# Attention operands split where they leave PSUM, keys turned by DMA, constants moved, and seven PSUM banks for output units

## The chip, the cores and the metric

The kernel is one program on one core of a Trainium2 chip. The core has TensorE (PE, with its weight loads shown apart as PEld), VectorE (DVE), ScalarE (ACT), GpSimd (POOL) and SyncE (SP). Each takes its own instructions in order. They meet through semaphores, and data comes and goes by DMAs, here nearly all issued from SP's queue. PE writes its results to PSUM, which has eight banks; DVE and ACT read them from there ("evacuate" them) into SBUF. The metric is the device time of the whole program in microseconds, lower is better.

## What is computed

The reference is one inference step of a decoder with two layers, on a prompt of 2048 tokens and on 8 sequences with 4 new tokens each (32 sample rows), with a model width of 1024:

```python
proj = h @ w_in                                   # layer 0; h = rmsnorm(x)
qa, fa, ia, ga, qb, kb, vb, gb, fb = _split(proj, [512]*4 + [512]*4 + [4])
o_a, s_a = gated_linear_chunked(...)              # linear attention with per-channel decay, 4 heads of 128
o_b = fox_attend(hb(qb), kb_h, vb_h, log_fb)      # softmax attention with forget bias, 4 heads of 128
out = concat([norm(o_a) * silu(ga), o_b * silu(gb)]) @ w_out
```

`fox_attend` on the prompt is causal attention with logits `q.k * scale + c_t - c_s`, where `c` is the running sum of log forget gates. On the samples it also reads 16 pages of 128 cached rows for each sequence. Layer 1 is another gated linear attention (GLA, 4 heads, keys of 128, values of 256), with its own input and output projections. The keys and values of layer 0 are outputs too, in fp32.

Every fp32 projection is done as three fp16 matmuls: each operand is split into a high part `hi = fp16(x)` and a low part `lo = fp16(x - hi)`, and `hi*hi + hi*lo + lo*hi` is accumulated in fp32 (`mm3`, lines 593 to 597). Attention does the same with Q, K, V and the probabilities.

## The kernel before, in words

The prompt is worked on in two halves of 1024 tokens; the 32 sample rows go with the first half. The stages follow each other on PE:

- Layer 0's input units (0 to 875 us in the profile). A unit is one block of 256 weight columns: fetch, measure, scale and split the weights, then project. `phase_even` runs 16 units for each half in the order v0 g0 qf0 qf1 Bq0 Bg0 v1 g1 qf2 qf3 Bq1 Bg1 Bk0 Bv0 Bk1 Bv1. `A` names belong to the linear attention, `B` names to softmax attention, and the last digit of B units is a pair of heads. Linear-attention heads (`lin_attn`) are mixed between the units by `mux`, which deals out the instructions of two generators by their costs: head 3 runs beside Bg1, Bk0 and Bv0.
- Softmax attention (875 to 1300 us). `fox_prompt` goes through 16 groups (a head and 512 query rows). `scores` computes logits and probabilities for four blocks of 128 rows, `values` transposes the probabilities on PE and multiplies them with V, one group behind. `fox_sample` is mixed in: it reads 256 pages of the cache through a pool of 25 buffers, turns the key pages on PE (`pkt`) and multiplies (`sc`, `pv`).
- Output units of layer 0 (1300 to 1500 us), then layer 1's input units with GLA heads, then its output units. Units 0 to 3 of a layer and half are `out_units(hf, layer)`.

The order inside an engine's queue is not written out by hand: a planner takes the traced instructions in order with a model of their durations, and `issue_after(x)` places the instructions traced inside it, those on x's engine, behind x. Tiles come from pools by tag with a number of buffers; a tile that reuses a buffer waits for its last readers.

The places that the change touches:

- `proj_tm` (line 608) projects with tokens on PSUM's partitions, two token tiles (256 rows) to a bank of tag `pj`; its `evac` callback moves the result out. There are three `pj` banks, two `gr`, two `o` and one `st`. The linear attention uses `gr`, `st` and `o`.
- `mk_bq` (line 980): Q's projection leaves PSUM by one ACT copy with a scale (line 990) and goes to DRAM in fp32 (`qTd`), already with the head's channels on partitions.
- `mk_bkv` (line 1000): K and V leave PSUM by one DVE multiplication (line 1019) into a `c2` tile (four buffers), which is stored as the output. V is stored a second time to `vd`. K is turned by four PE transposes per pair of tiles (line 1044) in a `gr` bank, leaves it by an ACT copy (line 1048) and is stored to `kTd`.
- In `fox_prompt`, `loads` (line 1348) fetches a group's Q, K and V in fp32 into `raw` tiles, issued while the group before is worked on, and `split` (line 1357) makes the fp16 parts: ACT copies, POOL subtracts (lines 1329 to 1331). V is also scaled on ACT. The splits stand behind the last exponential and the last turned key page.
- `more_consts` (line 162) makes masks and constants for later stages. It is traced inside the first unit after v0; on ACT its work stands behind the unit's second tanh, on DVE behind nothing.
- `out_units` (line 1805) runs `proj_tm` on `w_out`; DVE adds the residual (lines 1825 and 1831) as it empties the bank.

Of the kernel before, what the change touches and what calls it, by code (L numbers as in the profile page):

```python
# [123 lines left out]
class Kern:  # L124
    def __init__(self, ctx, tc, ins, outs):
        self.ctx, self.tc, self.nc = ctx, tc, tc.nc
        self.i, self.o = ins, outs
        self.loaded = {}


    def consts(self):
# [21 lines left out]
        self.qTd = dp.tile([NH, P, NTOK], F32, name="qTd")  # L153
        self.kTd = dp.tile([NH, P, NTOK], F32, name="kTd")
        self.sgd = dp.tile([NH, P, NTOK], F32, name="sgd")
        self.vd = dp.tile([NTOK, 512], F32, name="vd")
# [451 lines left out]
    def proj_tm(self, pps, act, W, hf, evac, nm, width=256, pairs=True):  # L608
# [3 lines left out]
        for g in range(0, len(tl), per):  # L612
# [6 lines left out]
            ps = pps.tile([P, per, width], F32, tag="pj", name=f"pt_{nm}{g}")  # L619
# [284 lines left out]
    def even_half(self, hf, act, wpool, wp, pps, npool, S):  # L904
# [95 lines left out]
        def mk_bkv(hp, which):  # L1000
# [3 lines left out]
            def run(W):  # L1004
# [5 lines left out]
                def ev(ps, g, cnt, m):  # L1010
# [5 lines left out]
                    if g % 2 == 0:  # L1016
                        held[:] = [wp.tile([P, 2, 256], F32, tag="c2", name=f"B{which}{hf}{hp}{g}")]
                    t = held[0]
                    nc.vector.tensor_scalar(t[:m, g % 2 : g % 2 + cnt], ps[:, :, :256], c, None, ALU.mult)
                    if m < P:  # L1020
                        dst = o[f"fox_{which}_s"][0].rearrange("b t h d -> (b t) (h d)")[:, cs]
                        nc.sync.dma_start(dst, t[:m, 0])
                        if which == "v":
                            nc.sync.dma_start(self.vd[T : T + TS, cs], t[:m, 0])
                    elif (g + cnt) % 2 == 0:
# [11 lines left out]
                    else:  # L1037
                        return
                    if which == "k":
                        pk = pps.tile([P, 2, 256], F32, tag="gr", name=f"BkT{hf}{hp}{g}")  # L1040
                        nt = 1 if m < P else 2
                        for j in range(2):
                            for c in range(nt):
                                nc.tensor.transpose(pk[:, j, c * P : c * P + m], t[:m, c, j * P : (j + 1) * P],
                                                    self.ident[:m, :m])
                        ks = wp.tile([P, 2, 256], F32, tag="c2", name=f"BkS{hf}{hp}{g}")
                        wd = nt * m
                        nc.scalar.activation(ks[:, :, :wd], pk[:, :, :wd], AF.Copy, scale=self.fsc["k", hp][0])
                        dc = T if m < P else hf * HALF + g * P
                        nc.sync.dma_start(  # L1050
                            self.kTd[2 * hp : 2 * hp + 2, :, dc : dc + wd].rearrange("h p t -> p h t"), ks[:, :, :wd])
# [23 lines left out]
    def phase_even(self):  # L1075
# [4 lines left out]
        with pool("act", side="right") as ap, pool("w", side="right") as w0, pool("wl", side="right") as wp1, \  # L1080
# [7 lines left out]
            self.scales2, self.ready, self.fsc, self.logit, self.v_undo = {}, {}, {}, {}, {}  # L1088
# [23 lines left out]
            for hf in range(2):  # L1112
# [11 lines left out]
                if hf == 0:  # L1124
# [26 lines left out]
                    with tc.issue_after(self.last_x.ins), tc.issue_after(self.last_a.ins), \  # L1151
                            tc.issue_after(self.last_th.ins):
# [146 lines left out]
    def phase_fox(self):  # L1299
# [5 lines left out]
        if True:  # L1305
            fx = Pool(f0, {"vh": 5, "vl": 5, "P": 17, "th": 4, "tl": 4, "sg": 3, "y": 1},
                      Pool(f1, {"raw": 6, "caus": 1, "qh": 2, "ql": 2, "kh": 5, "kl": 5, "cb": 2, "st1": 12, "cm": 2}))
# [9 lines left out]
    def load(self, fx, src, nm):  # L1317

        r = fx.tile([P, 512], F32, tag="raw", name=f"raw_{nm}")
        self.nc.sync.dma_start(r.rearrange("p (c d) -> p c d", d=src.shape[2]) if len(src.shape) == 3 else r, src)  # L1320
        return r

    def split(self, fx, r, nm, scale=None):

        nc = self.nc
        hi = fx.tile([P, 512], F16, tag=nm[0] + "h", name=f"h_{nm}")
        lo = fx.tile([P, 512], F16, tag=nm[0] + "l", name=f"l_{nm}")
        if scale is not None:
            nc.scalar.activation(r, r, AF.Copy, scale=scale)
        nc.scalar.activation(hi, r, AF.Copy)  # L1330
        nc.gpsimd.tensor_tensor(lo, r, hi, ALU.subtract)
        return hi, lo

    def fox_prompt(self, fx, pps, caus):

        nc = self.nc
        cbs, K, V, Q, SG, raw = {}, {}, {}, {}, {}, {}
# [10 lines left out]
        def loads(h, G):  # L1348
            gs = slice(G * 512, (G + 1) * 512)
            raw["q"] = self.load(fx, self.qTd[h][:, gs], f"q{h}{G}")  # L1350
            raw["k"] = self.load(fx, self.kTd[h][:, gs], f"k{h}{G}")
            bias(h, G)
            raw["v"] = self.load(fx, self.vd[gs, h * P : (h + 1) * P].rearrange("(c s) d -> s c d", s=P), f"v{h}{G}")
# [3 lines left out]
        def split(which, h, G):  # L1357

            with ExitStack() as st:
                for x in (self.last_exp, self.last_kt):  # L1360
                    if x is not None:
                        st.enter_context(self.tc.issue_after(x.ins))
                r = self.split(fx, raw[which], f"{which}{h}{G}", self.fsc["v", h // 2][0] if which == "v" else None)
# [825 lines left out]
```

## Time and profile before

| | us |
|---|---|
| median of 3 runs (2366.59 to 2371.02) | 2367.46 |
| the profiled execution | 2365.9 |
| its span in the trace | 2364.2 |
| PE busy in the span | 2265.2 |
| DVE busy | 1404.4 |
| ACT busy | 1090.3 |
| POOL busy | 818.6 |

The page gives the busy time of each engine, the costliest groups of instructions, and what each engine waited for. A matmul's end is modelled and neighbours overlap, so a matmul's listed duration (0.27 us for 128x256) is not the time that it takes from PE: the next one starts 0.109 us later. What PE loses is read from its idle time, and from the distance between starts. "Idle before, releaser" says which instruction ended the wait. TensorE's granted clock was 0.989 over the run.

### The profile page before, as it was taken

What the parts mean: (1) busy time and instruction counts of PE and PEld (TensorE: products, weight loads), DVE (VectorE), ACT (ScalarE), POOL (GpSimd) and SP (SyncE); (2) the same over time, 40 slices, a digit from 0 to 9 for tenths busy, and PEclk for the clock granted to TensorE, in tenths of its full rate; (3) what the DMA queues carried; (4) which work ended last, traced back from release to release, by engine and by line L of the source; (5) the groups of instructions that cost most, each with busy time, mean ns of one, the idle gap of its engine ahead of it and who ended that gap; (6) DMA issues with size and microseconds to landing.
All of it is one profiled execution on the core that took longest, in us unless ns stands there. A gap on an engine that the chain in (4) does not pass through costs nothing. (4 is left out here: it accounts for less than half of the span.)

```text
span 2364.2 us, 58202 instructions
## 1 busy us (share of the span) xinstructions
PE 2265.2 (96%) x23124; PEld 1613.1 (68%) x23124; DVE 1404.4 (59%) x3225; ACT 1090.3 (46%) x2372; POOL 818.6 (35%) x858
## 2 busy tenths in 40 slices
PE   6999999999999999999999999999899999999998
PEld 5667667864655875655445888777677666666887
DVE  6656557536664538666767444366675655557554
ACT  5434343333333226556667543436545545545333
POOL 3133324112212226234557345144452422222223
PEclk9999999999999999999999999999999999999999
DMA  6231334755441267776873867633234431115453
GB/s 191 73 89 59 100 109 146 196 157 148 145 123 56 75 196 239 239 256 198 280 239 117 278 197 249 148 96 108 79 117 101 107 103 57 48 55 166 152 194 149
DMA packets 358004, 344.89 MB, mean 146 GB/s; under 512 B 90994, under 2 KB 300723, under 8 KB 357731
## 3 DMA queue, kind: packets, MB, share of 16 engines
q1 hardware_dynamic: 356226, 336.64, 46.8%
q8 instruction: 182, 2.98, 0.5%
q0 software_dynamic: 1504, 4.52, 0.5%
q14 instruction: 92, 0.75, 0.1%
HBM read 248.73 MB, written 79.63 MB: 139 GB/s over the span
## 5 line engine op out<-in xcount | busy, mean ns | idle before, releaser
L595 PE MATMUL pt_o<-w_o,act 128*128 128x256 f16 x1024 | 281.1, 274 | 8.2 <-DVE xo L1825 6.6
L597 PE MATMUL pt_o<-w_o,act 128*128 128x256 f16 x1024 | 281.0, 274 | 3.8 <-DVE act L1784 3.7
L596 PE MATMUL pt_o<-w_o,act 128*128 128x256 f16 x1024 | 281.1, 275 | 1.5 <-POOL w_o L356 1.5
L597 PEld LDWEIGHTS <-act 128*128 128x128 f16 x2304 | 227.3, 99 | 39.4 <-DVE act L1784 5.1
L596 PEld LDWEIGHTS <-act 128*128 128x128 f16 x2304 | 227.3, 99 | 38.5 <-issue 8.4
L595 PEld LDWEIGHTS <-act 128*128 128x128 f16 x2304 | 227.4, 99 | 35.9 <-issue 3.4
L761 POOL TENSOR_TENSOR kA<-kA,fA 128x512 f32<-128x512 f32 (+1 forms) x56 | 79.5, 1419 | 190.1 <-PE gl_A L727 141.9
L595 PE MATMUL pt_Cv<-w_Cv,act 128*128 128x256 f16 (+1 forms) x512 | 141.4, 276 | 0.0
L597 PE MATMUL pt_Cv<-w_Cv,act 128*128 128x256 f16 (+1 forms) x512 | 141.3, 276 | 0.0
L596 PE MATMUL pt_Cv<-w_Cv,act 128*128 128x256 f16 (+1 forms) x512 | 141.3, 276 | 0.0
L761 POOL TENSOR_TENSOR kC<-kC,fC 128x512 f32<-128x512 f32 (+1 forms) x56 | 83.6, 1493 | 153.8 <-PE gl_C L727 102.5
L1392 ACT ACTIVATE L<-L,nm,kc 128x512 f32<-128x512 f32 (+3 forms) x160 | 118.2, 741 | 33.5 <-DVE nm L1390 27.8
L1400 POOL TENSOR_SCALAR L<-L,nm 128x512 f32<-128x512 f32 (+3 forms) x160 | 99.0, 632 | 64.5 <-DVE nm L1396 23.9
L1427 ACT ACTIVATE th<-pt 128x512 f16<-128x512 f32 (+3 forms) x159 | 80.5, 528 | 64.5 <-PE pt L1420 63.6
L1428 DVE TENSOR_TENSOR tl<-pt,th 128x512 f16<-128x512 f32 (+3 forms) x159 | 94.6, 609 | 21.4 <-ACT th L1427 20.5
L1420 PE MATMUL pt<-ident,L 128*128 128x128 f32 x544 | 91.2, 279 | 7.1 <-POOL L L1400 4.2
L1420 PEld LDWEIGHTS pt<-ident,L 128*128 128x128 f32 x544 | 66.6, 143 | 33.3 <-DVE tl L1428 8.3
L1544 PEld LDWEIGHTS pkt<-ident,pgcache_fox_k 128*128 128x128 f32 x512 | 57.4, 141 | 42.7 <-issue 25.1
L1877 ACT ACTIVATE vC<-pt_Cv,kc 128x512 f32<-128x512 f32 (+1 forms) x40 | 23.9, 598 | 129.9 <-PE pt_Cv L597 129.9
L1544 PE MATMUL pkt<-ident,pgcache_fox_k 128*128 128x128 f32 x512 | 75.1, 278 | 7.3 <-DVE kts L1548 5.1
L1825 DVE SCALAR_TENSOR_TENSOR xo<-pt_o,kc,xo 128x512 f32<-128x512 f32 x48 | 35.8, 748 | 62.0 <-PE pt_o L597 57.2
L597 PE MATMUL pt_Av<-w_Ai,act 128*128 128x256 f16 x256 | 70.9, 277 | 1.5 <-DVE act L591 1.5
(957 smaller groups left out, 6788.5 us busy)
## 6 DMA issues: line engine op xcount, KB each, us to landing
pgcache_fox_k<-in_cache_fox_k SPq DMA_DIRECT2D x128, 256.0 KB, 4.4
pgcache_fox_v<-in_cache_fox_v SPq DMA_DIRECT2D x128, 256.0 KB, 4.3
yr<-yT SPq DMA_DIRECT2D x16, 1024.0 KB, 7.2
x1d<-xo SPq DMA_DIRECT2D x48, 256.0 KB, 4.1
wr_Aqf<-in_w_in_even SPq DMA_DIRECT2D x64, 128.0 KB, 3.2
wr_o<-in_w_out_even SPq DMA_DIRECT2D x32, 256.0 KB, 6.0
xo<-in_x_prompt SPq DMA_DIRECT2D x32, 256.0 KB, 4.2
wr_Cv<-in_w_in_odd SPq DMA_DIRECT2D x32, 256.0 KB, 3.8
```

The lines of the kernel that those rows point to most:

```text
L595: nc.tensor.matmul(ps, lh[0], rh[0], start=first, stop=False)
L596: nc.tensor.matmul(ps, lh[0], rh[1], start=False, stop=False)
L597: return nc.tensor.matmul(ps, lh[1], rh[0], start=False, stop=last)
L761: nc.gpsimd.tensor_tensor(kv[:, :, 0], kv[:, :, 0], t1.to_broadcast([P, nb, w]), ALU.mult)
L1392: self.last_exp = nc.scalar.activation(lt[:, :w], lt[:, :w], AF.Exp, bias=nm[:, 0:1], scale=ib, accum_out=nm[:, 2 + j : 3 + j])
L1400: nc.gpsimd.tensor_scalar(lt[:, :w], lt[:, :w], nm[:, 1:2], 2.0**14, ALU.mult, ALU.mult)
L1420: nc.tensor.transpose(pt[:, w : w + P], rows[b][s // 4][0][:, (s % 4) * P : (s % 4 + 1) * P], self.ident)
L1427: nc.scalar.activation(th[:, a:w], pt[:, a:w], AF.Copy),
L1428: nc.vector.tensor_tensor(tl[:, a:w], pt[:, a:w], th[:, a:w], ALU.subtract)))
L1544: nc.tensor.transpose(pk[:, j * P : (j + 1) * P], pgs[j][:, h * P : (h + 1) * P], self.ident)
L1825: nc.vector.scalar_tensor_tensor(t[:m, :cnt], ps, c, t[:m, :cnt], ALU.mult, ALU.add)
L1877: r = nc.scalar.activation(v[h][:, g : g + cnt], ps[:, :, :256], AF.Copy, scale=c)
```

## The change

1. K and V. Where a bank of K or V leaves PSUM, ACT now also writes `hi` in fp16 with a combined scale (`cu`, one new column for each of K and V and pair of heads), and DVE writes `lo = ps * cu - hi`. Both go to DRAM (`kd`, `vd`) beside each other, in token order. The PE transposes of K for the prompt are gone, with the ACT copy of their result. The fp32 outputs are made as before. The 32 sample rows keep their old path, with small DRAM tiles of their own (`qs`, `ks`, `vs`).
2. Q. The ACT copy writes `hi` in fp16, DVE writes `lo`, both into the same `c2` tile, stored to `qd`. The last segment of the first half holds 32 sample columns, which take a copy and a tile of their own.
3. Attention. `loads` fetches the fp16 parts as they are used. K comes by a transposing DMA (512 tokens by 256 columns for a group). `load` and `split` are gone, and with them the `raw` tiles; the pools are now `q2` 3, `k2` 6 and `v2` 6 tiles of 2 KB for each partition.
4. `more_consts` stands behind the second silu's last DVE operation (`last_si`) instead of its tanh on ACT.
5. The output units take PSUM tiles in the turn `pj gr pj o pj gr o`, seven banks, except those of layer 1's first half, which run beside a linear-attention head.

```diff
-    def proj_tm(self, pps, act, W, hf, evac, nm, width=256, pairs=True):
+    def proj_tm(self, pps, act, W, hf, evac, nm, width=256, pairs=True, banks=("pj",)):
...
-            ps = pps.tile([P, per, width], F32, tag="pj", name=f"pt_{nm}{g}")
+            ps = pps.tile([P, per, width], F32, tag=banks[self.bank % len(banks)], name=f"pt_{nm}{g}")
+            self.bank += 1
...
-        nc.vector.scalar_tensor_tensor(dst, th[:, :n], 1.0, dst, ALU.add, ALU.mult)
+        self.last_si = nc.vector.scalar_tensor_tensor(dst, th[:, :n], 1.0, dst, ALU.add, ALU.mult)
...
-                            nc.scalar.activation(t[:, :m], ps, AF.Copy, scale=self.fsc["q", hp][0])
-                            store_cols(self.qTd[h], t, c0, m)
+                            up, few = self.fsc["q", hp][0], max(0, c0 + m - HALF)
+                            u = t.bitcast(F16).rearrange("p (x t) -> p x t", x=2)[:, :, : m - few]
+                            nc.scalar.activation(u[:, 0], ps[:, : m - few], AF.Copy, scale=up)
+                            nc.vector.scalar_tensor_tensor(u[:, 1], ps[:, : m - few], up, u[:, 0], ALU.mult,
+                                                           ALU.subtract)
+                            dc = hf * HALF + c0
+                            nc.sync.dma_start(self.qd[h][:, :, dc : dc + m - few], u)
...
                     nc.vector.tensor_scalar(t[:m, g % 2 : g % 2 + cnt], ps[:, :, :256], c, None, ALU.mult)
+                    if m == P:
+                        u = held[1]
+                        for j in range(cnt):
+                            src = ps[:, j, :256].rearrange("p (h d) -> p h d", h=2)
+                            hi, lo = (u[:, g % 2 + j, :, x] for x in range(2))
+                            nc.scalar.activation(hi, src, AF.Copy, scale=self.cu[which, hp])
+                            nc.vector.scalar_tensor_tensor(lo, src, self.cu[which, hp], hi, ALU.mult, ALU.subtract)
...
-                        if which == "v":
-                            dst = self.vd[pg * P : (pg + 2) * P, cs].rearrange("(g s) d -> s g d", s=P)
-                            nc.sync.dma_start(dst, t)
+                        dst = {"k": self.kd, "v": self.vd}[which][pg * P : (pg + 2) * P, 2 * hp : 2 * hp + 2]
+                        nc.sync.dma_start(dst.rearrange("(g s) h x d -> s g (h x d)", s=P),
+                                          u.rearrange("p g h x d -> p g (h x d)"))
-                    if which == "k":
+                    if which == "k" and m < P:
...
                     with tc.issue_after(self.last_x.ins), tc.issue_after(self.last_a.ins), \
-                            tc.issue_after(self.last_th.ins):
+                            tc.issue_after(self.last_si.ins):
                         self.more_consts(wp)
...
-            raw["q"] = self.load(fx, self.qTd[h][:, gs], f"q{h}{G}")
-            raw["k"] = self.load(fx, self.kTd[h][:, gs], f"k{h}{G}")
+            q, k, v = (fx.tile([P, 1024], F16, tag=x + "2", name=f"{x}2_{h}{G}") for x in "qkv")
+            q, k = (x.rearrange("p (x t) -> p x t", x=2) for x in (q, k))
+            v = v.rearrange("p (c x d) -> p c x d", c=4, x=2)
+            nc.sync.dma_start(q, self.qd[h][:, :, gs])
+            nc.sync.dma_start_transpose(k, self.kd[gs, h].rearrange("t x d -> t (x d)"))
...
-                    elif b == 2:
-                        split("q", *groups[j + 1])
-                        split("k", *groups[j + 1])
-                    elif b == 3:
-                        split("v", *groups[j + 1])
...
+        self.cu[which, hp] = self.kcol()
+        nc.vector.tensor_scalar(self.cu[which, hp], c, up, None, ALU.mult)
...
+                    lambda W: self.proj_tm(pps, act, W, hf, ev, f"o{layer}{hf}{u}", pairs=not done or u < 3,
+                                           banks=("pj", "gr", "pj", "o", "pj", "gr", "o") if free else ("pj",)))
```

More of the change, by code (lines that the diff above doesn't have):

```diff
@@ L127, in __init__ @@
         self.i, self.o = ins, outs
-        self.loaded = {}
+        self.loaded, self.bank = {}, 0
     def consts(self):
@@ L1315, in phase_fox @@
                 drain(until(self.prompt, FOX_P, self.fox_sample(fs, pps), FOX_S))
[L1317 to L1332, printed above, removed]
     def fox_prompt(self, fx, pps, caus):
         nc = self.nc
-        cbs, K, V, Q, SG, raw = {}, {}, {}, {}, {}, {}
+        cbs, K, V, Q, SG = {}, {}, {}, {}, {}
         self.turns = []
@@ L1448, in fox_prompt @@
         loads(0, 0)
-        for x in "qkv":
-            split(x, 0, 0)
         pv, ns = iter(()), 0
@@ L1455, in fox_prompt @@
                 rows.append((yield from scores(h, G, b)))
-                if j + 1 < len(groups):
-                    if b == 0:
-                        loads(*groups[j + 1])
-                    elif b == 2:
-                        split("q", *groups[j + 1])
-                        split("k", *groups[j + 1])
-                    elif b == 3:
-                        split("v", *groups[j + 1])
+                if j + 1 < len(groups) and b == 0:
+                    loads(*groups[j + 1])
                 for _ in range(ns // 4):
@@ L1524, in fox_sample @@
         vn = one([TS, 512], "vn")
-        for t, d in ((qs, self.qTd), (kn, self.kTd), (sgs, self.sgd)):
-            nc.sync.dma_start(t, d[:, :, T : T + TS].rearrange("h p t -> p h t"))
-        nc.sync.dma_start(vn, self.vd[T : T + TS])
+        for t, d in ((qs, self.qs), (kn, self.ks), (sgs, self.sgd[:, :, T : T + TS])):
+            nc.sync.dma_start(t, d.rearrange("h p t -> p h t"))
+        nc.sync.dma_start(vn, self.vs)
         with self.tc.issue_after(self.last_l.ins):
@@ L1810, in mk @@
         def mk(u):
[L1811 removed]
+            cs, free = slice(u * 256, (u + 1) * 256), (hf, layer) != (0, 1)
             undo = [self.kcol()] + ([self.kcol()] if layer == 0 and hf == 0 else [])
@@ L1840, in mk @@
                                    scaler="pool" if (hf, layer, u) == (0, 0, 0) else None),
-                    lambda W: self.proj_tm(pps, act, W, hf, ev, f"o{layer}{hf}{u}", pairs=not done or u < 3))
+                    lambda W: self.proj_tm(pps, act, W, hf, ev, f"o{layer}{hf}{u}", pairs=not done or u < 3,
+                                           banks=("pj", "gr", "pj", "o", "pj", "gr", "o") if free else ("pj",)))
         return [mk(u) for u in range(4)]
```

52 lines of the change are left out of this document (24 added, 28 removed).

## The prediction

> **What bounds the kernel now.** I read the page's head first, then the table by stages (windows of the span), then the chain of waits, each engine's waits, and the timeline where a wait was large.
>
> ```profile
> span 2364.2 us, 58202 instructions
> PE 2265.2 (96%) x23124; PEld 1613.1 (68%) x23124; DVE 1404.4 (59%) x3225; ACT 1090.3 (46%) x2372; POOL 818.6 (35%) x858
> ```
>
> PE is busy for 96% of the span: a microsecond counts if it is PE work removed, or one of the 99 us in which PE stands. By stages (columns: stretch, its length, busy time of PE, PEld, DVE, ACT, POOL with instructions, granted clock, DMA share, GB/s):
>
> ```profile
> 0.00:58.00 58.00, 39.10 (x298) 30.69 (x299) 40.07 (x109) 33.70 (x71) 18.19 (x51) 0.97 0.66 191
> 357.80:430.50 72.70, 70.02 (x912) 59.89 (x910) 56.45 (x127) 29.70 (x68) 29.53 (x25) 0.98 0.56 170
> 875.00:1300.00 425.00, 396.34 (x2784) 231.69 (x2784) 298.49 (x933) 275.54 (x621) 213.53 (x322) 0.98 0.70 227
> 1400.00:1510.00 110.00, 104.25 (x927) 89.48 (x925) 45.44 (x77) 39.97 (x64) 41.60 (x26) 0.98 0.82 232
> ```
>
> PE's idle time lies where the change works: 18.9 us at the start (0 to 58), 28.7 us in attention (875 to 1300), 5.8 us in output units (1400 to 1510). The stretch 357.8 to 430.5 (first half's Bk0 and Bv0 beside a linear-attention head) shows the reverse: PE 70.0 of 72.7 us, DVE already 56.5 of them. That is where DVE work is added.
>
> **1. Keys turned by DMA instead of PE.** Per pair of token tiles PE ran four transposes of Bk.
>
> ```profile
> 836.80 0.60 PE L1044 MATMUL BkT<-ident,Bk 128*128 128x128 f32 x4
> 848.15 0.60 PE L1044 MATMUL BkT<-ident,Bk 128*128 128x128 f32 x4
> 848.59 0.27 PE L595 MATMUL pt_Bk<-w_Bk,act 128*128 128x256 f16 x1
> 848.70 0.27 PE L596 MATMUL pt_Bk<-w_Bk,act 128*128 128x256 f16 x1
> L1044 PE MATMUL BkT<-ident,Bk x68: 221/273/421, 375.0 to 854.2; 128*128 128x128 f32 x64, 32*128 32x32 f32 x4
> L1048 ACT ACTIVATE BkS<-BkT,kc x18: 294/687/690, 375.7 to 854.5; 128x512 f32<-128x512 f32 x16, 128x64 f32<-128x64 f32 x2
> L1019 DVE TENSOR_SCALAR Bk<-pt_Bk,kc x16: 731/750/751, 369.2 to 851.1; 128x512 f32<-128x512 f32 x16
> ```
>
> The row says 0.60 us, but the next matmul starts 0.44 us after the transposes (848.15 to 848.59): matmuls overlap, and 0.44 us is what they hold. 64 of the 68 go, 16 groups: 16 x 0.44 = **-7.0 us**, nearly all of it on the path, because PE does not wait in Bk. The four 32-row ones of the samples stay.
>
> **2. Splitting at PSUM.** 64 tiles of 128x256 (two pairs of heads, K and V, 16 tiles each) get an ACT copy to fp16 and a DVE subtraction. Nearest rows, the same pair of operations from PSUM, and a wider subtraction:
>
> ```profile
> L591 DVE SCALAR_TENSOR_TENSOR act<-nt,g_even,act 128x256 f16<-128x256 f32 x32 | 13.8, 472 | 1.9 <-ACT act L590 1.8
> L590 ACT ACTIVATE act<-nt,g_even 128x256 f16<-128x256 f32 x32 | 13.5, 481 | 11.2 <-PE nt L455 10.9
> L1428 DVE TENSOR_TENSOR tl<-pt,th 128x512 f16<-128x512 f32 x112 | 75.6, 686 | 20.3 <-ACT th L1427 19.6
> ```
>
> DVE +64 x 0.472 = 30.2 us; ACT +64 x 0.481 - 16 x 0.687 = +19.8 us. Q keeps its ACT copy and gains a DVE subtraction per segment, 0.47 to 0.69 us each by those rows: some 12 us over 20 segments. The stores keep their bytes (two fp16 for one fp32) and their number; four one-column operations in the scales are nothing.
>
> Cover: a pair of tiles takes PE 5.2 us (48 matmuls 0.109 us apart) and its evacuation goes from 0.75 us of DVE to 0.75 + 2 x 0.47 = 1.7; three pj banks hide that as long as DVE has room. In 357.8 to 430.5, Bk0 adds 4 pairs x 0.94 and Bv0 8 tiles x 0.47: 7.5 us, so DVE rises from 56.5 to 64.0 of 72.7 us. There the linear attention's own steps queue behind the subtractions on DVE, PE takes its instructions in order and waits for them. Lower end 0 (a queue full of ready work), upper end 7.5 here and as much again in the second half, 15. I take half of the first, **+4 us**: the second half's twin (790 to 833) has DVE at half load. The Trainium skill, "PSUM — Partial Sum Buffer", section "PSUM bank collisions raise a hardware error", says that two engines must not touch one bank's quadrant at the same time, reads included. By that the copies and subtractions follow each other and a pair holds its bank 2.7 us, still under 5.2; the term would stay, and the rows' 1.8 us of DVE waiting for act over 32 pairs agree that the hand-over is cheap.
>
> At the hand-over to attention the last V tile leaves PSUM two subtractions later; the first score matmul already waits 1.0 us for it:
>
> ```profile
> PE s L595 <- DVE Bv L1019: 1.0, 1, 1.0
> ```
>
> **+1 us** (0 to 2).
>
> **3. Attention without splits.** Per group ACT did three copies and a scaling, POOL three subtractions:
>
> ```profile
> L1330 ACT ACTIVATE h_k<-raw_k x16: 612/616/643, 863.7 to 1246.3; 128x512 f16<-128x512 f32 x16
> L1329 ACT ACTIVATE raw_v<-raw_v,kc x16: 704/710/722, 868.8 to 1251.6; 128x512 f32<-128x512 f32 x16
> L1331 POOL TENSOR_TENSOR l_k<-raw_k,h_k x16: 1151/1157/1168, 864.9 to 1249.6; 128x512 f16<-128x512 f32 x16
> PE pkt L1544 <- DVE kts L1548: 5.1, 6, 1.7
> PE pt L1420 <- POOL L L1400: 4.2, 4, 2.3
> PE fo L595 <- ACT th L1427: 3.3, 4, 1.8
> PE s L596 <- POOL l_k L1331: 1.2, 2, 0.7
> ```
>
> ACT loses 16 x (3 x 0.616 + 0.710) = 40.9 of 275.5 us, POOL 16 x 3 x 1.157 = 55.5 of 213.5. PE is the bound, so only its waits can be won: POOL's L, th and l_k are 4.2 + 3.3 + 1.2 = 8.7 us. Lower end 0: DVE, whose 298.5 us are untouched, ends the next wait (kts 5.1 us stays). Upper end 15, half the stage's 28.7 idle us. I take the waits named, nearly whole, **-8 us**.
>
> The loads: q and v come as before. Keys come by a DMA transpose on SP's queue. Nearest rows (16 blocks of 128x128 each, a group's K has 8) against the plain load:
>
> ```profile
> L565 SPq DMA_TRANSPOSE act<-xs x17: 1282/2489/3579, 1417.4 to 1836.8; - x17
> DMA to landing us min/median/max: 4.0/5.3/7.1
> L1320 SPq DMA_DIRECT2D raw_k<-kTd x16: 332/372/428, 860.2 to 1217.3; - x16
> SPq L1514 <- PE pkt L1544: 49.6, 41, 13.4
> ```
>
> SP is held some 1.2 to 2.5 us instead of 0.37, 16 times: at most 34 us more on a queue on which the page reads stand behind. I price it at **0**: SP's own waits for a page buffer (49.6 us) say that pages run ahead until PE frees one, and K is loaded a group (425 / 16 = 27 us on the mean) ahead, against 5.3 to land. Without that cover it costs up to 2.1 us a group. The Trainium skill, "VectorE: DVE Perf Modes", section "Rules for kernel authors", speaks against this step: TensorE for a 128x128 transpose where PSUM will do. Its figures, 390 ns there and 1309 ns by DMA, make an estimate of 25 us for the 64 transposes of PE and 168 us for the 128 fp16 blocks by DMA; were both on the path, the sum below would be -18 + 7 - 25 + 168 = +132 us. By the rows a transpose holds PE 0.11 us, and DMA time is on the path only through SP's queue, which is rival (c).
>
> **4. VectorE's constants behind the second unit.** Now DVE takes them in the middle of the first normalisations:
>
> ```profile
> 35.10 0.16 DVE L175 TENSOR_TENSOR lb<-lb 128x4 f32<-128x4 f32 x1 [2.99 <-DMA lb<-in_lb_logits]
> 35.18 0.15 DVE L406 TENSOR_SCALAR rst_n<-nss 128x1 f32<-128x1 f32 x1
> 39.45 0.69 PE L455 MATMUL nt<-ident,nx 128*128 128x128 f32 x2 [4.00 <-DVE act L591]
> DVE g_hgrn L168 <- DMA g_hgrn<-in_hgrn_gain: 1.1, 1, 1.1
> DVE mlev L213 <- POOL mtmp L210: 3.3, 4, 1.1
> 105.06 1.79 DVE L673 COPY_PREDICATED scT<-mdiag,gd_A 32x256 f32<-32x256 int8 x4 [8.88 <-PE gd_A L670]
> ```
>
> DVE stands 2.99 us for lb's load; rst_n, ready meanwhile, starts behind it, and PE then waits 4.00 us. I take 3 us of that and 1 of the 1.1 us wait for g_hgrn: **-4 us**, between 0 (the loads of x end the wait instead) and 5.5. The constants, some 5 us, land on DVE near 70 us; before the masks' first use at 105 it stands 8.9 us, which covers them.
>
> **5. Seven banks for output units.**
>
> ```profile
> L595 PE MATMUL pt_o<-w_o,act 128*128 128x256 f16 x1024 | 281.1, 274 | 8.2 <-DVE xo L1825 6.6
> PE pt_o L595 <- DVE xo L1825: 5.7, 4, 2.0
> ```
>
> PE waits 6.6 us in all for a pj bank, 5.7 of them between 1400 and 1510. Six banks ahead instead of two cover each (2.0 us at most), but weights and normalisation beside them may be next late: **-4 us**, between 0 and 6.6. The Trainium skill, "Perfetto Trace Analysis", section "Matmul Optimizations", would have all eight banks used; read as a promise it gives the whole 6.6, so 2.6 us more. What xo's row holds is all there is to win.
>
> **The sum.** -7 +4 +1 -8 -4 -4 = -18 us. It is made against the profiled execution, 2365.9 us (span 2364.2), 1.6 us under the median of the three runs shown, 2367.46. So 2347.9 there, and 2349.5 on the median: **2349 us**, 0.8% faster.
>
> **The rivals.** (a) Only PE work and DVE's order count: attention gains nothing, since DVE ends its waits anyway. kts' 5.1 us speak for it, POOL's and ACT's waits against. -18 + 8 = -10: 2357 us; with the banks given back too, 2361.
> (b) DVE becomes the bound where operands leave PSUM: the 7.5 us in each half reach PE whole, 15 instead of 4, and attention gains nothing: -18 + 11 + 8 = +1, 2368 us, no change. DVE at 88% of 72.7 us speaks for it, the half-empty second half against.
> (c) Slower: SP's queue decides. A K transpose issues ahead of page reads, pages come late, PE stands before pkt and pv. At the full 2.1 us, 16 times, it is +34, and -18 + 34 = +16: 2383 us. It decides from 18 / 16 = 1.1 us a group on, measurably slower from 1.4; 49.6 us of SP waiting for free pages speak against it. The rule of the Trainium skill under 3 is on its side.
> (d) More: attention gains 15 and the start and the banks their upper ends: -7 - 15 - 5.5 - 6.6 = -34, DVE's additions hidden: 2333 us.
>
> **How the numbers follow.** Forecast, 2340 to 2355: 0.50. (a) 0.18, (d) 0.12, (b) 0.09, (c) 0.11. Changes below 0.2% (4.7 us) cannot be told here from none. The range runs from (d) to just short of (b), 2332 to 2366, leaving out (c) and half of (b). Faster holds the forecast, (d) and nearly all of (a), 0.79; the rest of (a) and most of (b) are within 0.2%, 0.08; (c) and the rest of (b) slower, 0.13.
>
> **What would show it.** Right: no BkT rows but the samples'; Bk's pairs 5.2 us apart on PE, not 5.7; no 4 us wait near 35 us; DVE's constants near 70 us; no xo in PE's waits; ACT near 235 and POOL near 158 us of busy time in attention, PE's idle time there near 20 us. Wrong: new PE waits for DVE or POOL kA between 357 and 430 us (b), PE waiting before pkt or pv for pages with SP busy in DMA_TRANSPOSE (c), kts and tl taking over the waits of L and th (a). A K transpose that takes several microseconds on SP would undo the forecast.

## The result, and the profile after

The change made the kernel slower: 2374.26 us in the median against 2370.31 us of the kernel before on the same chip (20 runs each). The ratio on record is 1.0025 with a 95% interval of 1.0016 to 1.0034; it is not the quotient of the two medians, which is 1.0017. The prediction was 2349 us, between 2332 and 2366. Single executions of the changed kernel lie up to 7 us from their median (2367.18 to 2380.64), and the two profiled ones lie further apart than the medians: 2379.06 us after, 4.8 over its median, 2365.9 before, 4.4 under the median given here. So the traces say where time went, and the ratios how much.

The head of the page after; the busy times before were PE 2265.2, DVE 1404.4, ACT 1090.3 and POOL 818.6 us:

```profile
span 2377.4 us, 58131 instructions
...
PE 2254.8 (95%) x23060; PEld 1607.1 (68%) x23060; DVE 1441.6 (61%) x3313; ACT 1073.0 (45%) x2360; POOL 760.2 (32%) x810
```

Every engine moved as it was meant to: PE lost 10 us of work, POOL 58, ACT 17, and DVE gained 37. The span is longer all the same, so PE stands more. To see where, compare the first and last starts of PE's groups (view of the groups of instructions by tile; "891.0 to 1089.7" are the first and last start). Before:

```profile
L595 PE MATMUL pf_Ag<-act,w_Ag x160: 312/313/379, 56.4 to 663.6; 128*128 128x352 f16 x96, 128*128 128x512 f16 x64
...
L595 PE MATMUL s<-h_k,h_q x160: 216/379/607, 874.2 to 1277.4; 128*128 128x512 f16 x112, 128*128 128x128 f16 x16, 128*128 128x256 f16 x16, 128*128 128x384 f16 x16
...
L1544 PE MATMUL pkt<-ident,pgcache_fox_k x512: 272/273/332, 891.0 to 1089.7; 128*128 128x128 f32 x171
...
L1683 PE MATMUL pv<-pgcache_fox_v,pT x256: 592/592/1061, 1105.4 to 1253.2; 128*16 128x512 f32 x128
...
L595 PE MATMUL pt_o<-w_o,act x1024: 269/273/421, 1299.3 to 2355.0; 128*128 128x256 f16 x171
...
L595 PE MATMUL pt_Cv<-w_Cv,act x512: 272/273/421, 1481.5 to 2099.0; 128*128 128x256 f16 x128, 128*128 128x272 f16 x43
```

After:

```profile
L598 PE MATMUL pf_Ag<-act,w_Ag x160: 312/313/379, 50.0 to 659.8; 128*128 128x352 f16 x96, 128*128 128x512 f16 x64
...
L598 PE MATMUL s<-k,q x160: 216/379/634, 863.7 to 1279.5; 128*128 128x512 f16 x112, 128*128 128x128 f16 x16, 128*128 128x256 f16 x16, 128*128 128x384 f16 x16
...
L1530 PE MATMUL pkt<-ident,pgcache_fox_k x512: 272/273/330, 888.8 to 1137.3; 128*128 128x128 f32 x171
...
L1669 PE MATMUL pv<-pgcache_fox_v,pT x256: 589/592/1061, 1154.6 to 1272.0; 128*16 128x512 f32 x128
...
L598 PE MATMUL pt_o<-w_o,act x1024: 269/273/421, 1303.2 to 2368.1; 128*128 128x256 f16 x171
...
L598 PE MATMUL pt_Cv<-w_Cv,act x512: 272/273/434, 1483.4 to 2110.8; 128*128 128x256 f16 x128, 128*128 128x272 f16 x43
```

The change is 6.4 us ahead when the second unit begins (50.0 against 56.4), 10.5 ahead when attention begins (863.7 against 874.2), and 3.9 behind when the output units begin: attention took 439.5 us instead of 425.1. The output units win 2.0 of this back, and from the first to the last Cv unit the lag grows from 1.9 to 11.8 us. Inside attention the key pages are turned (`pkt`) until 1137 us instead of 1090, and the value pages (`pv`) are multiplied in 117 us instead of 148.

What PE waited for in attention (total us, times, longest), after (`mx` are the row maxima that DVE takes as it makes the logits `L`; `th` and `tl` are the high and low parts of the transposed probabilities):

```profile
PE pv L1669 <- DMA pgcache_fox_v<-in_cache_fox_v: 20.6, 15, 3.7
PE s L598 <- DVE mx L1378: 14.4, 5, 9.3
PE fo L599 <- DVE tl L1422: 6.2, 5, 3.5
```

The first, the value pages, is not in the list of before; the second, mainly a single stand at attention's start, was 2.5 us there. The value pages are asked for 36 to 41 us later than before. Their first and last issue, before and then after:

```profile
L1514 SPq DMA_DIRECT2D pgcache_fox_v<-in_cache_fox_v x128: 332/333/1550, 1054.6 to 1231.3; - x128
```

```profile
L1500 SPq DMA_DIRECT2D pgcache_fox_v<-in_cache_fox_v x128: 332/333/1285, 1095.5 to 1267.4; - x128
```

Key and value pages share the pool of 25 buffers, and SP stood 63.2 us between 940 and 1150 for `pkt` to free one. Once PE multiplies, SP asks for a value page about every microsecond, 51 in 50.9 us, of which it waits 7.3 for `pv` to free a buffer:

```profile
1155.67 50.93 SPq L1500 DMA_DIRECT2D pgcache_fox_v<-in_cache_fox_v  x51
```

And the stand at the start, in the timelines of DVE and SP:

```profile
877.18 0.29 DVE L1378 CUSTOM_DVE_ANT_0 L<-s,cb 128x128 f32<-128x128 f32 x1 [8.92 <-DMA vd<-Bvs]
```

```profile
863.27 2.67 SPq L1352 DMA_TRANSPOSE k<-kd  x1
...
870.48 1.84 SPq L1513 DMA_DIRECT2D vn<-vs  x1
872.58 0.96 SPq L1500 DMA_DIRECT2D pgcache_fox_k<-in_cache_fox_k  x2
873.64 0.38 SPq L1058 DMA_DIRECT2D vd<-Bvs  x1
```

By the program's memory layout the second probability tile lies where the last fp16 parts of V (`Bvs`) were. They are written by 867.8, but SP issues their store at 873.6, behind loads for later; DVE stands 8.9 us for its landing, and PE behind DVE.

### The profile page after: what moved, and what is told of

Its sections match the earlier page's. It is cut to its first block, busy times and chain, and to the rows that moved or that the text cites. A ratio compares the mean times of both kernels' runs of the same rounds, so it can differ in the third digit from the quotient of the medians.

```text
span 2377.4 us, 58131 instructions
## 1 busy us (share of the span) xinstructions
PE 2254.8 (95%) x23060; PEld 1607.1 (68%) x23060; DVE 1441.6 (61%) x3313; ACT 1073.0 (45%) x2360; POOL 760.2 (32%) x810
## 4 chain that ended last, share of the span: by engine, by line
PE 75%; DVE 9%; DMA 7%; ACT 3%; issue 2%; SPq 2%; POOL 1%; DVEq 0%; POOLq 0%; ACTq 0%
PE pt_o L599 4%; PE pt_o L598 4%; PE pt_o L600 4%; PE pkt L1530 2%; PE pt L1414 2%; PE pt_Cv L598 2%; PE pt_Cv L599 2%; PE pt_Cv L600 2%; DMA pgcache_fox_v<-in_cache_fox_v 2%; PE sc L1588 1%; PE pf_Ag L600 1%; PE pf_Ag L599 1%; PE pf_Ag L598 1%; PE pf_Bq L600 1%; PE pf_Bq L598 1%
## 5 line engine op out<-in xcount | busy, mean ns | idle before, releaser
L1530 PEld LDWEIGHTS pkt<-ident,pgcache_fox_k 128*128 128x128 f32 x512 | 58.9, 141 | 39.5 <-issue 24.7
L1364 POOL TENSOR_TENSOR cm<-cb,caus 128x128 f32<-128x128 f32 x64 | 29.0, 454 | 143.7 <-DVE mx L1378 88.7
L598 PE MATMUL pt_Bk<-w_Bk,act 128*128 128x256 f16 x256 | 70.6, 276 | 1.5 <-DVE Bvs L1042 1.2
```

Of the source, the lines that this page charges most:

```text
L598: nc.tensor.matmul(ps, lh[0], rh[0], start=first, stop=False)
L1364: self.last_cm = nc.gpsimd.tensor_tensor(cm, cb[:, tb * P : (tb + 1) * P], caus, ALU.add)
L1530: nc.tensor.transpose(pk[:, j * P : (j + 1) * P], pgs[j][:, h * P : (h + 1) * P], self.ident)
```

## The experiments

All ratios are those on record, to the kernel before, from runs on the same chip as the kernel named; "us" is the ratio's distance from 1 times 2366.

| kernel | median | ratio (95% interval) | us |
|---|---|---|---|
| the change | 2374.26 | 1.0025 (1.0016 to 1.0034) | +5.9 |
| e1 change, PE's order put back | 2361.75 | 0.9979 (0.9970 to 0.9989) | -5.0 |
| e2 parts 1 to 3 alone | 2384.29 | 1.0079 (1.0060 to 1.0097) | +18.7 |
| e3 constants alone | 2358.09 | 0.9964 (0.9950 to 0.9978) | -8.5 |
| e4 banks alone | 2366.47 | 1.0000 (0.9989 to 1.0012) | 0 |
| e5 e1 and other memory | 2360.50 | 0.9984 (0.9970 to 0.9998) | -3.8 |
| e6 e5 with three banks | 2361.69 | 0.9988 (0.9975 to 1.0000) | -2.8 |
| e7 e1 with K by a plain load | 2358.48 | 0.9969 (0.9957 to 0.9981) | -7.3 |
| e8 e5, norm loads on ACT | 2379.60 | 1.0059 (1.0043 to 1.0075) | +14.0 |
| e9 e2 with PE's order | 2374.24 | 1.0041 (1.0026 to 1.0055) | +9.7 |
| e10 before, without the order | 2378.27 | 1.0058 (1.0045 to 1.0072) | +13.7 |
| e11 e5, SP's order at the start | 2351.06 | 0.9940 (0.9927 to 0.9952) | -14.2 |
| e12 e11 with the old memory | 2351.85 | 0.9948 (0.9936 to 0.9960) | -12.3 |

### The order of the page stream: e1, e10, e7, e9

The theory: in the kernel before, `split` stood behind `last_kt`, the last turned key page (front part, "the places that the change touches"). It made the next group's scores wait until the samples' pages had been turned, so the page stream ran ahead. When `split` was deleted, this order went with it. The rival was the prediction's case (c), SP's queue held by the transposing DMAs.

e1 adds only an order on PE to the changed kernel:

```diff
+                self.last_turn = nc.tensor.transpose(pk[:, j * P : (j + 1) * P], ...)
...
-                self.last_pe = self.mm3(ps[:, :w], q, ...)
+                with ExitStack() as st:
+                    if j == 0 and behind[0] is not None:
+                        st.enter_context(self.tc.issue_after(behind[0].ins))
+                    self.last_pe = self.mm3(ps[:, :w], q, ...)
+                    behind[0] = None
...
+                if b == 2:
+                    turned = self.last_turn
+                if b == 3:
+                    behind[0] = turned
```

> The changed kernel, with PE's first score matmul of each attention group placed behind the last key page turned (pkt) when the group before was at its third block. No wait is added, only PE's order. Theory A (order): the removed splits stood behind the last turned page and held the next group's scores back, so the page stream of the samples stayed ahead; without them the scores run ahead, the last pkt moves from 1090 to 1137 us and the value pages are squeezed into the last 120 us of attention, where PE waits 20.6 us for them. With the order put back those waits fall under 5 us, the last pkt is back near 1090, attention is some 10 to 15 us shorter and the kernel near 2361 us. Theory B (SP's queue): the DMA transposes of K hold up the page reads on SP; then the waits for value pages stay near 20 us whatever PE's order, and the kernel stays near 2374. Theory C (neither): the waits move to DVE (kts, tl), and the kernel lies between, near 2370.

e10 does the reverse to the kernel before, one word, with K still turned by PE and no transposing DMA of K. What goes is an order on ACT: the splits no longer stand behind ACT's copy of the last turned page.

```diff
-                for x in (self.last_exp, self.last_kt):
+                for x in (self.last_exp,):
```

> The kernel before with one order removed and nothing else: its splits no longer stand behind the last turned key page on ACT. Every operation, load and store of before is kept, K is turned by PE and read by a plain DMA. Theory A (order): PE's scores run ahead of the page stream as in the changed kernel, the value pages are squeezed to the end and PE waits for them: 10 to 20 us over the kernel before. Theory B: the order costs nothing without K's transposing DMAs and the later loads: within 3 us of the kernel before.

The groups by tile, and PE's waits, of e1:

```profile
L1538 PE MATMUL pkt<-ident,pgcache_fox_k x512: 272/273/332, 884.8 to 1081.2; 128*128 128x128 f32 x171
...
L1676 PE MATMUL pv<-pgcache_fox_v,pT x256: 589/592/1061, 1096.9 to 1246.2; 128*16 128x512 f32 x128
```

```profile
PE pv L1676 <- DMA pgcache_fox_v<-in_cache_fox_v: 1.2, 2, 0.6
```

And of e10:

```profile
L1544 PE MATMUL pkt<-ident,pgcache_fox_k x512: 272/273/476, 888.3 to 1137.1; 128*128 128x128 f32 x171
...
L1683 PE MATMUL pv<-pgcache_fox_v,pT x256: 589/592/862, 1155.9 to 1272.9; 128*16 128x512 f32 x128
```

```profile
PE pv L1683 <- DMA pgcache_fox_v<-in_cache_fox_v: 20.5, 17, 3.2
```

The two sides agree. With the order, the wait for value pages falls from 20.6 to 1.2 us and `pkt` ends at 1081; without it the old kernel shows the same 20.5 us wait and the same last `pkt` at 1137 as the changed one, and is 13.7 us slower. e1 lies 10.9 us under the change by the ratios. The order is shown to be the cause of the late pages; K's transposes are not needed for it.

e7 prices those. On e1, K of each group comes by a plain load of the same bytes; it leaves out the turning, so attention's values differ:

```diff
-            nc.sync.dma_start_transpose(k, self.kd[gs, h].rearrange("t x d -> t (x d)"))
+            nc.sync.dma_start(k.rearrange("p x t -> p (x t)").rearrange("p (c y) -> p c y", c=4),
+                              self.kd[gs, h].rearrange("(c s) x d -> s c (x d)", s=P))
```

> The kernel of e1, with K of each attention group loaded by a plain DMA of the same bytes (the keys then lie untransposed, so attention's values are others than the reference's; all the work is done). It prices the transposing DMAs. Theory A (hidden, as I predicted): SP holds each for about 1 us more than a plain load, 16 us in all, under its own waits for free pages; only the start of attention, where four of them stand before the last V store, gets shorter: 2357 to 2361 us against 2361.75. Theory B (rival c): transposes hold up page reads or DMA engines all through attention: 10 us or more under e1, below 2352.

SP's issues of K, in the changed kernel:

```profile
L1352 SPq DMA_TRANSPOSE k<-kd x16: 1226/1294/2665, 847.7 to 1146.9; - x16
```

In e7:

```profile
L1352 SPq DMA_DIRECT2D k<-kd x16: 360/406/1320, 845.9 to 1194.2; - x16
```

The median hold of SP falls from 1.29 to 0.41 us, 14 us over 16 loads, and the kernel by 2.3 us (0.9969 against 0.9979, in overlapping intervals). Theory A; case (c)'s mechanism falls, though its symptom, PE standing before `pv`, was there. The Trainium skill, "VectorE: DVE Perf Modes", section "Rules for kernel authors", prefers TensorE for a 128x128 transpose where a result in PSUM will do. By the figures of that page the prediction had estimated 132 us over the kernel before, were all of it on the path; e7 leaves 2 us for K's DMAs over plain loads, by the ends of the intervals under 8.

e9 is e2 (parts 1 to 3, with `issue_after(self.last_th.ins)` and `banks=("pj",)` as before) with the order of e1. First e2, then e9:

> Parts 1 to 3 alone (operands split where they leave PSUM, K by a transposing DMA); the constants stay behind the second tanh and the output units keep their three banks. If the parts add up, this is the changed kernel plus the 6.4 us that the start gained and whatever the banks are worth: 2380 us if the banks are worth nothing, 2385 if they keep 5. If the start's gain is lost again on the way (the normalisation only meets its next wait), it is near 2375.

> Parts 1 to 3 alone, as in e2 (constants and banks as before), with PE's order put back as in e1. It gives what the split, K's DMA transposes and the loads are worth when the page stream keeps its place. My prediction's parts 1 to 3 sum to -10 us. Theory A (order was all of e2's +17 us): the K transposes' 7 us off PE remain, less the crowding at PSUM (+4) and the later start of attention (+5): 2364 to 2370, the kernel before. Theory B (the loads cost by themselves): still 6 us or more over the kernel before.

The order takes 9 us off e2, but e9 stays 9.7 over the kernel before: theory B by its number. Its trace has the start's stand too (PE waited 14.5 us for `mx`, 8.9 at once), so the order was not all of it. e9 lies 14.6 us over e1, whose only other parts are the constants and the banks, worth 8.5 and 0 alone. The 6.1 us between are about as much as the four intervals together allow (some 6), and the two traces show no such gap: e9 is 8.9 us behind e1 when the second unit begins (58.0 against 49.1) and 9.1 at the end. The granted clock of e9 is lower as well, 0.9858 in the mean of its runs against 0.9884 in e1's, an estimated 6 us on some 2250 us of busy PE. Whether the parts add up is not settled.

### The start of attention: e5, e12, e11

e5 lays attention's small tiles ahead of the probability tiles, so that the second of them no longer lies on `Bvs`:

```diff
+            for x in ("th", "tl"):
+                fx.tile([P, 512], F16, tag=x, name=f"{x}_at")
```

> The kernel of e1 (PE's order put back), and the th and tl tiles of attention laid in memory ahead of the probability tiles P, so that the second P tile no longer lies where the last V parts (Bvs) wait for their store. In e1 DVE's second logits operation stood 8.2 us for the landing of vd from Bvs, and PE 8.2 us behind it before the fourth score block. Theory A: that wait was the hand-over's price; it goes, and the kernel is 5 to 8 us under e1, near 2355 us. Theory B: the store's place takes another wait in its stead (the load of V of group 0 stands behind the same store on SP), and the gain is under 3 us: 2359 to 2362.

e11 adds an order on SP: loads of groups 3 and later, the samples' loads and the first eight pages stand behind the last V store. e12 is e11 without e5's edit.

```diff
-                        nc.sync.dma_start(dst.rearrange("(g s) h x d -> s g (h x d)", s=P), ...)
+                        self.last_vd = nc.sync.dma_start(dst.rearrange("(g s) h x d -> s g (h x d)", s=P), ...)
...
+                    with ExitStack() as st:
+                        if j >= 2:
+                            st.enter_context(self.tc.issue_after(self.last_vd.ins))
+                        loads(*groups[j + 1])
...
+        with self.tc.issue_after(self.last_vd.ins):
             for t, d in ((qs, self.qs), (kn, self.ks), ...):
...
+                if len(asked) < 8:
+                    st.enter_context(self.tc.issue_after(self.last_vd.ins))
```

> The kernel of e5, and at attention's start SP issues the last V store ahead of the loads of groups 3 and later, the sample's loads and the first key pages. In e5's trace DVE still stood 4.7 us for that store to land, and PE 4.1 us behind it. Theory A (the store is the wait): PE loses under 3 us before the first pkt, where e5 lost 9.5 to DVE, and the kernel is 4 to 6 us under e5 (ratio to before 0.9984): near 0.996, 2356 to 2358 us. Theory B (what DVE waits for is next the bias rows or the V loads behind it): ratio 0.998 or more, 2361.

> The kernel of e11 with the memory of attention's tiles as in the changed kernel: the second probability tile again lies where the last V parts wait for their store, but SP issues that store ahead of the loads, as in e11. e5 (memory alone) was worth nothing over e1, e11 (memory and SP's order) about 10 us. Theory A (the store's place on SP's queue is what counts): 2352 to 2356 us, ratio 0.994 to 0.996. Theory B (both are needed, as either wait alone keeps the start): 2360, ratio 0.998.

The timeline of e5:

```profile
871.40 0.38 SPq L1058 DMA_DIRECT2D vd<-Bvs  x1
...
874.93 0.69 DVE L1384 CUSTOM_DVE_ANT_0 L<-s,cb 128x512 f32<-128x512 f32 x1 [4.68 <-DMA vd<-Bvs]
```

Of e12:

```profile
865.73 0.36 SPq L1058 DMA_DIRECT2D vd<-Bvs  x1
...
868.08 0.29 DVE L1382 CUSTOM_DVE_ANT_0 L<-s,cb 128x128 f32<-128x128 f32 x1 [1.92 <-DMA vd<-Bvs]
```

Moving the tiles only moved the wait: in e5 the store is issued no sooner, and the fifth probability tile, which still overlaps the end of `Bvs` by 352 bytes, stands 4.7 us for it. Issued 0.03 us after its data is complete (865.22 + 0.48 us of the last subtraction, 865.73), as in e12, it leaves DVE 1.9 us, 6.3 less than in e1. e12 is worth 7.3 us over e1, e11 9 to 10 over e1 and e5. The store's place on SP's queue was the cost. Other memory alone gained nothing (e5 against e1), and on top of the new order 1.9 us (e11 against e12), inside the intervals. e11, at 2351.06 us, and e12 beat both kernels, e11 by 14 us over before.

What is left of attention in e12 (stretch, its length, busy time of PE, PEld, DVE, ACT, POOL, clock, DMA share, GB/s):

```profile
862.60:1284.90 422.30, 394.18 (x2786) 232.24 (x2784) 299.07 (x937) 245.86 (x563) 161.00 (x275) 0.98 0.73 229
```

Against 425.1 us from the first score to the first output matmul before, attention gained 2.8 us in all; in e11's trace (861.5 to 1286.5) it gained 0.1. ACT lost 30 us and POOL 52 of their work there, and PE still stands 28.1 us, where it stood 28.7 (prediction's stage table). So case (a) comes near in its outcome, attention hardly gains. Its reason is not borne out: DVE's `kts` (the turned key pages copied out of PSUM) and `tl` did not take over the waits, they fell from 5.9 and 5.5 us before to 4.0 and 2.6 in e11.

### The constants: e3

```diff
-                            tc.issue_after(self.last_th.ins):
+                            tc.issue_after(self.last_si.ins):
```

> The kernel before, with the constants placed behind the second silu's last operation on DVE and nothing else. My prediction said -4 us; the two traces show -6.4 us at the end of the first unit, kept to the end of layer 0's first half. Kept to the end: 2370.3 - 6.4 = 2364. Given back in attention, where transfers set the pace: 2367 to 2370.

0.9964 is -8.5 us, between -5 and -12. It agrees with the 6.4 us of the traces, and by the ratio is kept to the end. e3's own trace has 5.9 us at the second unit (50.5 against 56.4) and 3.4 at the end, from an execution 4.4 us above e3's median. In the changed kernel DVE takes the constants from 61.8 us on, beside the second unit:

```profile
61.78 0.17 DVE L171 TENSOR_SCALAR g_hgrn<-g_hgrn 128x4 f32<-128x4 f32 x1
...
61.92 0.16 DVE L178 TENSOR_TENSOR lb<-lb 128x4 f32<-128x4 f32 x1
```

### The banks: e4, e6, e8

e4 adds to the kernel before only the turn of seven banks. e6 is e5 with `banks=("pj",)`.

> The kernel before, with seven banks for the output units and nothing else. Prediction: -4 us, 2366. Theory A (given back): the output units gain some 5 us, but layer 1's first unit then waits as long for the turned rows of the normalisation (act from xs by DMA), which is what sets its start: 2369 to 2371. Theory B (kept): 2365. Theory C (a loss): the output units take the gr and o banks that the next stage's transposes use, and layer 1 starts later than before: 2372 to 2374.

> The kernel of e5 with three pj banks for the output units as before. Banks alone were worth nothing in e4 (ratio 1.000): the output units gained 9.0 us in its trace and layer 1's first unit gave 8.5 of them back, behind nine transposing DMAs of the normalisation that SP works off in a row. If that holds here too, e6 equals e5 within 2 us. If the banks help where the start of layer 1 is reached at another time, e6 is 4 to 6 us over e5.

Both say nothing gained: ratio 1.0000 alone, and e5 and e6 1 us apart. e4's trace shows why. Its output units end 10 us sooner than before's, the first Cv unit starts 8.3 sooner, the second 1.6. In between PE waits for the normalised rows, which come by transposing DMAs. Waits and issues of e4 there:

```profile
SPq L1825 <- DMA x1d<-xo: 16.6, 4, 5.2
PE pt_Cv L595 <- DMA act<-xs: 3.2, 2, 1.6
```

```profile
1467.62 3.38 SPq L565 DMA_TRANSPOSE act<-xs  x1
1472.22 2.23 SPq L565 DMA_TRANSPOSE act<-xs  x1
1475.17 6.02 SPq L565 DMA_TRANSPOSE act<-xs  x2
```

And before, the first of them in that stretch:

```profile
1469.11 3.58 SPq L565 DMA_TRANSPOSE act<-xs  x1
```

PE was ready 8 to 10 us sooner, the transposes came 1.5 us sooner. SP, in order, stands ahead of them 16.6 us for residual stores (`x1d` from `xo`) to land, whose tiles the next loads need; then each transpose holds it 2 to 3 us. The changed kernel has the same wait (PE 4.8 us for `act` from `xs`), at the place where its lag grew.

e8 takes those loads off SP (on e5):

```diff
-            self.nc.sync.dma_start_transpose(act.both[:, :, :, c0 : c0 + n]...
+            self.nc.scalar.dma_start_transpose(act.both[:, :, :, c0 : c0 + n]...
```

> The kernel of e5, with the transposing loads of layer 1's normalised rows (act from xs, 17 of them) issued by ACT's queue instead of SP's. In e1 and e4 they run back to back on SP, behind SP's waits of 15 us for residual stores to land, and set the pace of layer 1's first unit. Theory A: away from that queue they start earlier and the banks' gain is kept, 3 to 7 us under e5. Theory B: ACT is held 2 to 4 us by each, and its own work (evacuations of the first unit) comes late: no gain or a loss of up to 10 us.

Groups by tile and ACT's waits in e8:

```profile
L568 ACTq DMA_TRANSPOSE act<-xs x17: 1312/2563/10059, 1405.0 to 1842.0; - x17
```

```profile
ACT vC L1875 <- issue: 44.7, 1, 44.7
```

Theory B, by more than its bound: the loads hold ACT 2.6 us each in the median, once 10.1, and the evacuation of Cv starts late. By the ratios 17.7 us over e5. The Trainium skill, "DMA: Bandwidth & Descriptors", section "DMA Transpose (X-bar)", lets plain transposes be issued by Sync or Scalar only. So a plain transpose has no third queue to go to here. Whether the banks' gain can be kept stays open.

## Why the prediction was wrong, step by step

**1. Keys off PE, -7.0, and 2. PSUM crowding, +4: right together.** From the end of the first unit to attention's start the traces moved by 10.5 - 6.4 = -4.1 us, where -3 was summed. Without the transposes the last four pairs of Bk take 21.3 us on PE (820.5 to 841.8), where they took 22.6 (828.2 to 850.8): 1.3 us less, as forecast for the three groups of transposes between them. The first half shows the crowding: PE stood for ACT and DVE in the linear attention's steps and for the split itself, 8.2 us in all from 293 to 470 us, against 3.4 before from 300 to 475. After:

```profile
PE st_A L872 <- ACT kts_A L848: 2.1, 1, 2.1
PE o_A L885 <- DVE S L891: 1.5, 1, 1.5
PE pt_Bk L598 <- DVE Bvs L1042: 1.2, 1, 1.2
```

DVE's load there, 57.0 of the 72.7 us from 350.0 on, stayed under the 64.0 forecast. The second half had room, as said: PE stood 2.0 us from 730 to 864, 2.4 before from 737 to 874. Case (b) falls.

**The hand-over to attention, +1: mis-sized.** It was priced by the last V tile's subtractions, a wait of DVE. What came was a store's landing: 9.3 us at once on PE. The step counted the instructions added on DVE and not what SP's planned order would put between the last subtraction and its store, nor that a later tile reuses that memory. Before's trace had the same wait at 1.35 us (`vd` from `Bv`, ahead of a later block's logits). Of two stores from one fp32 tile one became a store of an fp16 tile that is complete later.

**3. Attention without splits, -8: the step that failed.** It failed twice. First, of the 8.7 us of waits that it meant to win (POOL's `L`, ACT's `th`, POOL's `l_k`), 5.9 are still there in e11, with no split left to make them:

```profile
PE s L598 <- DVE mx L1384: 5.1, 7, 2.7
PE pt L1420 <- POOL L L1400: 3.8, 1, 3.8
...
PE fo L598 <- ACT th L1427: 2.1, 6, 0.5
```

With the order and the store put right the stage gained 0.1 us (e11) to 2.8 (e12). PE's stand for `mx` is still longer there than before, 5.1 and 7.4 us against 2.5, with 1.0 more for `Bv` then. If that is the start's doing alone, the splits were worth some 2 to 7 us; no run separates the two, and -8 is not reached either way.

Second, and dearer, the step priced the splits' place in the order at nothing. The text before the prediction says that they "stand behind the last exponential and the last turned key page", and the sum treats that as no work. It kept the page stream ahead, worth 13.7 us in e10 and 10.9 in e1. The sentence that gave cover, "SP's own waits for a page buffer (49.6 us) say that pages run ahead until PE frees one", read its row in the wrong direction: a queue that waits 49.6 us for `pkt` to free a buffer has its pace set by where PE places `pkt`, and that was what the change moved.

**K's transposing DMA, 0: right**, to within e7's 2.3 us.

**4. Constants, -4: too small.** -6.4 in the traces, -8.5 by e3. The stand that was priced went as forecast: PE's waits of `nt` for `act` at the start fell from 5.2 us to 1.2. The rest of the gain was in waits that the step did not name, 1.5 us of it in `pt_Av` behind `act`; its upper end of 5.5 is not worked out there.

**5. Banks, -4: wrong.** The output units did gain (9 us in e4's trace, over the 6.6 that the `xo` row held), and layer 1's start gave it back. The prediction named that possibility in one clause ("normalisation beside them may be next late"), but took only 2.6 of the 6.6 us off for it; rival (a) alone let the whole be given back, at 2361 us.

By the parts measured: -6.4 for the start, -4.1 to attention, +7 to +9 for its start, +11 to +14 for the order, 0 for the banks, some -3 for the splits. That is +4.5 to +9.5, against +5.9 by the ratio on record. That the sum meets it is in part luck, because the profiled pair divides its +13.2 us otherwise: -10.5 up to attention, +14.4 in it and +9.3 behind it (-2.0 in the output units, +8.3 between the first and the second Cv unit, the rest later). From the output units to the end e1's trace loses 4.8 us on before's and e12's nothing. What the 9.3 us are is open.

## What to carry to other kernels

An instruction does work and it also holds a place: before deleting one, list what was ordered behind it and what it was ordered behind, and ask which stream gets ahead without it. A queue that waits for a consumer's buffers, as SP did here, is no cover: the consumer sets its pace. Where a stage is made faster, look at the transfers that the next stage needs and at what stands ahead of them on their queue: if they do not move, the gain ends there.

## What the runs showed of the hardware

- A transposing DMA holds the engine that issues it: 1.3 us of SP in the median for 512 tokens by 256 fp16 columns, against 0.41 for the plain load, and 2.6 us of ACT in the median, once 10.1, for the normalised rows (e8). On SP, with slack, 14 us of this cost some 2; on ACT the 17 loads of the normalised rows cost 17.7.
- Value pages of 256 KB were issued at one per us (51 in 50.93 us, with 7.3 us of waits for `pv` to free a buffer). With the pool's 25 buffers, `pv` squeezed from 148 into 117 us stood 20.6 us for them.
- Order alone moved the kernel by 13.7 us (e10): one anchor less on ACT, with every operation, load and store the same.
- The granted clock was lower in a stretch where PE stood much: in the kernel before, 0.94 from 882 to 912 us with PE busy for 24.7 of 30 us, 1.00 from 912 to 962 with 48.3 of 50. Over whole runs the two slowest kernels have the lowest clock, 0.985 in e2 and 0.984 in e8 in the mean of their runs, and the two fastest the highest, 0.990 in e11 and e12. No run separates whether the stands lower the clock or the clock lengthens the run.
